# A hybrid decoder layer on one core: the DeltaNet scan without u and w formed ahead, and two groups of loads moved ahead of their splits

## The chip, the cores and the metric

The kernel runs on one core of one Trainium2 chip. The metric is the device time of one execution in microseconds (us); the time before is the median of three runs. All names of engines are those of the profile: PE is TensorE's matmul, PEld its weight load, DVE is VectorE, ACT is ScalarE, POOL is GpSimd, SP is the SyncE queue, which issues nearly all DMAs of this kernel.

## The reference

One layer over 1024 tokens of width 1024: a norm, one combined projection, two mixers side by side (gated DeltaNet with 8 heads of 128, and a sparse attention with three branches), their gated sum through an output projection, and an MLP. The part that matters is the chunked delta rule of each DeltaNet head. The reference solves for u and w ahead and then scans the chunks:

```
u = triangular_solve(t_mat, vb)                    # t_mat = 1 + strictly lower (kb k^T * decay)
w = triangular_solve(t_mat, kb * exp(gc))
qk = (q k^T) * decay ; q_dec = q * exp(gc) ; k_end = k * exp(gc_last - gc)
for each chunk:
    v_new = u_c - w_c @ state
    o     = q_dec @ state + qk @ v_new
    state = state * g_last + k_end^T @ v_new
```

Everything is float32. The merge is `sigmoid(g_dn) * (o_dn @ W_dn) + sigmoid(g_ns) * (o_ns @ W_nsa)`, which then goes through `W_out`.

## The kernel before, in words

Large products are float32 values split in two parts (hi in ACT: `act(hi, src)`; lo in DVE: `src - hi`), with three 128x512 matmuls for each 128 rows of depth. The weights of such a product come 512 columns at a time through `unit`: a DMA into `wr` (or `a22` late in the program), the two-part split into `wh` and `wl`, out of a ring of five buffers (`WB`).

The program is laid out by hand on a line of steps: `at(step, rank, fn)` collects functions, and at the end they are run in order of step and rank. A framework then keeps the program's data dependencies, and sets each engine's own order; each engine takes its instructions strictly in that order. The stages, in order of time: projection of small columns and compressed keys (to 200 us), the eight DeltaNet heads (200 to 1035 us), the sparse stage of 32 items (1035 to 1543), the merge (1543 to 1650), output projection and MLP.

A head `head(h, s0)` takes 8 steps of projection (k, q, v, gate; two halves of 512 tokens each). One half of a projection is 24 matmuls into a tile `g`: `first` does 12 of them, and `conv` (or `gate`) the other 12 and then the short convolution on DVE and ACT. Between heads stand steps of `fill` projections, which the mixers need later: `fill_nb` (sparse keys, values, queries) and `fill_rows` (merge gates, stored to `gtd`). While these matmuls run, the head's delta rule goes on in small steps in between: `k_natural`, `k_turn`, `k_k`, `k_q` prepare keys, decay and qk; `blocks` and `inv_*`, `join_*`, `last_*` invert the triangular matrices of all chunks (the inverse, transposed, is `zs`); `u_w` forms u and w for four chunks at a time; `chunk` then does one chunk of 128 tokens: two matmuls with the state (`St`) against `wq` (w and the decayed q side by side), a subtraction on DVE (`vn`), the matmul `ke` with `vn` and the state's update on DVE, the matmul `qk` with `vn`, and the output row on ACT. There are 8 chunks to a head, and chunks of one head run during the projections of the next. `out_norm` and `out_turn` norm and transpose the head's rows and store them to `odd`.

In PSUM the chunk's tiles are named `c`, in a pool of two banks (`PL.pc`), which `out_turn` takes its transposes from too. The root of a norm (`rsqrt`) is a power on POOL. The product of q and decay, half of `wq`, is on POOL as well.

In the sparse stage `dn_rows(half)` loads the DeltaNet rows (`odd`) through the two staging tiles `ra` and `rb` and splits them into `oh` and `ol`; `dn_part` multiplies them by `w_proj_dn` between the items. Its last two columns (c = 6, 7 of the second half) are done after the items, with gates `ths`. Then pools are closed and opened (`pn`, `cq` go, `pw`, `py` come), `ns_rows` loads and splits the sparse rows (`ond` into `o`), and `ns_merge` multiplies them by `w_proj_nsa` into PSUM tiles named `V`.

Of the kernel before, what the change touches and what calls it, by code (L numbers as in the profile page):

```python
# [19 lines left out]
S = 1024  # L20
# [123 lines left out]
def body(ctx: ExitStack, tc: tile.TileContext, A, out):  # L144
# [246 lines left out]
    eg = PL.cq.tile([128, 8, NT], F32, name="eg")  # L391
# [3 lines left out]
    beg = PL.cq.tile([128, 8, NT], F32, name="beg")  # L395

    def gating():
# [44 lines left out]
        act(eg, gc, AF.Exp)  # L442
        V.tensor_tensor(beg, beta, eg, OP.mult)
# [187 lines left out]
    def head(h, s0):  # L631
# [11 lines left out]
        def conv(s, half):  # L643
# [3 lines left out]
            proj(ps, H["w", s], half, (4, 8))  # L647
# [30 lines left out]
        def k_turn(half):  # L678
            sl = S4[half]
            kn = H["kn", half]  # L680
            pt = flip(kn)
            kT = t4("kT", 2)
            act(kT, pt)
            H["kT", half] = kT
            kb = t4("kbe", 2)
            rows_by(kb, kn, beg[:, h, sl])
            H["kbe", half] = kb
# [5 lines left out]
            H["qk", half] = dt = t4("qk", 3)  # L693
# [59 lines left out]
        def k_q(half):  # L753
# [3 lines left out]
            w = pd.tile([128, 4, 2, 128], F32, name="wq", bufs=2)  # L757
            GP.tensor_tensor(w[:, :, 1], ac, H["gcB"].rearrange("p (t c) -> p t c", c=128)[:, S4[half]],
                             OP.mult)
            H["wq", half] = w  # L760

        def v_natural(half):
            ps = flip(H.pop(("ac", 2, half)))
            v_ = t4("vb", 2)
# [3 lines left out]
        def first(s, half):  # L768
            H["g"] = gtile()
            proj(H["g"], H["w", s], half, (0, 4))  # L770

        def gate(half):
            ps = H.pop("g")
            proj(ps, H["w", 3], half, (4, 8))
# [62 lines left out]
        def chunk(c):  # L837
# [3 lines left out]
            o, u, St = H["o", half], H["u", half], H.get("S")  # L841
            ps = PL.pc.tile([128, 2, 128], F32, name="c")
            if St is None:
                vn = u[:, i]
            else:
                wq = H["wq", half]
                mm(ps[:, 0], wq[:, i, 0], St, True, True)
                mm(ps[:, 1], wq[:, i, 1], St, True, False)
                vn = PL.p2.tile([128, 128], F32, name="vn", bufs=2)
                V.tensor_tensor(vn, u[:, i], ps[:, 0], OP.subtract)  # L850
            if c < 7:
                p2 = PL.pc.tile([128, 128], F32, name="c")
                mm(p2, H["ke", half][:, i, :], vn, True, True)
                H["S"] = Sn = PL.p2.tile([128, 128], F32, name="St", bufs=2)
                if St is None:
                    V.tensor_copy(Sn, p2)
                else:
                    V.scalar_tensor_tensor(Sn, St, H["gl"][:, c:c + 1], p2, op0=OP.mult, op1=OP.add)
            mm(ps[:, 1], H["qk", half][:, i], vn, St is None, True)
            act(o[:, i, :], ps[:, 1], AF.Copy, scale=H["rq", half][:, i:i + 1])  # L860
# [17 lines left out]
        for i, s in enumerate((1, 0, 2, 3)):  # L878
            at(s0 + 2 * i - 2, 2, prep, s)
            for half in range(2):  # L880
                at(s0 + 2 * i + half, 1, first, s, half)
                if s < 3:
                    at(s0 + 2 * i + half + 0.5, 1, conv, s, half)
                else:
                    at(s0 + 2 * i + half + 0.5, 1, gate, half)
        for half in range(2):
# [19 lines left out]
        at(s0 + 21.2, -1, out_norm, 1)  # L906
        at(s0 + 22.2, -1, out_turn, 1)

    def fill_rows(src, dst):
# [6 lines left out]
        def begin(half):  # L916
            w[1] = gtile()
            proj(w[1], w[0], half, (0, 4))

        def go(half):  # L920
            ps = w[1]
            proj(ps, w[0], half, (4, 8))
# [5 lines left out]
        def plan(s, half):  # L928
            at(s, 1, begin, half)
            at(s + 0.5, 1, go, half)  # L930
# [3 lines left out]
    def fill_nb(u):  # L934
# [11 lines left out]

        def go(t):
            tk = slice(t * 128, (t + 1) * 128)
            ps = gtile(256)
            gemm(ps, [(hh[:, k, tk], hl[:, k, tk], w[k // 2][0][:, k % 2], w[k // 2][1][:, k % 2])  # L950
                      for k in range(8)])
# [28 lines left out]
        def plan(s, j):  # L980
            for t in (2 * j, 2 * j + 1):
                at(s + t % 2 / 2, 1, go, t)
# [8 lines left out]
    for h in range(NDN):  # L991
# [3 lines left out]
        fills = gts if h == 7 else nbs[6:] if h == 6 else [nbs[h], gts.pop(0)]  # L995
# [5 lines left out]
    END, FULL = last + 24, last + 28  # L1001
# [340 lines left out]

    def dn_rows(half):
# [28 lines left out]
    for half in range(2):  # L1372
        at3(0.2 + 16 * half, dn_rows, half)
# [16 lines left out]

    shut("pn", "cq")
# [9 lines left out]
    rows_o, mixes, ks = [], [], {}  # L1401
# [27 lines left out]
    ths = []  # L1429
    for c in (6, 7):  # L1430
        ths.append(t512(PL.pw, "a12"))
# [339 lines left out]
```

## Time and profile before

| | us |
|---|---|
| median of 3 runs (2360.64 to 2361.92) | 2360.92 |
| profiled execution: its time | 2355.1 |
| profiled execution: its span | 2353.3 |
| PE busy (98% of the span) | 2306.0 |
| DVE busy (67%) | 1567.3 |
| ACT busy (49%) | 1155.6 |
| POOL busy (8%) | 184.2 |

The profiled execution's own time is 1.8 us above its span. "Busy" counts an instruction from its start to its modelled end; matmuls overlap, so that the time one really takes of PE is the distance from its start to the next start. Idle time of PE is listed where the next matmul started after the end of the last. Engines wait on each other by semaphores; a releaser named in a row is the one whose event came last.

### The profile page before, as it was taken

To read this page: it belongs to the slowest core of one execution; us is meant where nothing else is said; L and a number is where in the kernel's file an instruction comes from. 1 tells how busy PE (TensorE), PEld (TensorE's weight loads), DVE (VectorE), ACT (ScalarE), POOL (GpSimd) and SP (SyncE) were. 2 spreads that over 40 slices of the span, in tenths; PEclk is the share of its full clock that TensorE was granted. 3 is DMA by queue.
4 is the path that set the end of the run, shared out by engine and by line. 5 is a ranking of instruction groups with operands and counts; after the bars stand their busy time and mean duration, and the time that the engine had idled before them with its cause. 6 is when DMAs were issued, how large, how long until landed. Compare 5 with 4: busy or idle time off the path is not lost.

```text
span 2353.3 us, 43197 instructions
## 1 busy us (share of the span) xinstructions
PE 2306.0 (98%) x16257; PEld 1917.6 (81%) x16257; DVE 1567.3 (67%) x3742; ACT 1155.6 (49%) x2482; POOL 184.2 (8%) x198
## 2 busy tenths in 40 slices
PE   8999999999999999999999999999999999999999
PEld 5888988888988898886777777778878888888887
DVE  7676654747574748247777777645498777787775
ACT  4335353535444454337666666532465555544443
POOL 1021210101111121000010111100000000000000
PEclk9999999999999999999999999999999999999999
DMA  6421313131213221247342422065525443595333
GB/s 196 122 62 59 81 52 96 47 89 47 84 47 84 59 74 55 82 143 184 109 128 63 122 87 66 19 220 166 174 90 179 148 148 131 189 327 185 115 114 103
DMA packets 237378, 267.28 MB, mean 114 GB/s; under 512 B 76848, under 2 KB 128496, under 8 KB 237040
## 3 DMA queue, kind: packets, MB, share of 16 engines
q1 hardware_dynamic: 237168, 264.51, 36.1%
q8 instruction: 128, 2.10, 0.4%
q14 instruction: 82, 0.67, 0.1%
HBM read 190.02 MB, written 72.38 MB: 112 GB/s over the span
## 4 chain that ended last, share of the span: by engine, by line
PE 86%; DVE 6%; DMA 2%; issue 2%; ACT 1%; POOL 1%; SPq 0%; ACTq 0%; POOLq 0%; DVEq 0%
PE g L174 31%; PE V L174 20%; PE Q L174 12%; PE T L174 5%; PE s L174 5%; PE o L174 5%; PE S L174 2%; PE c L174 2%; PE m L174 1%; POOL ss L239 1%; PE tp L606 1%; DVE wl L274 1%; PE tp L174 1%; DVE junk L1238 0%; DVE acc L659 0%
## 5 line engine op out<-in xcount | busy, mean ns | idle before, releaser
L174 PE MATMUL g<-hh,wh 128*128 128x512 f32 (+1 forms) x816 | 335.9, 412 | 6.6 <-ACT hh L171 6.5
L174 PE MATMUL g<-hl,wh 128*128 128x512 f32 (+1 forms) x816 | 322.8, 396 | 0.1
L174 PE MATMUL g<-hh,wl 128*128 128x512 f32 (+1 forms) x816 | 322.4, 395 | 0.0
L171 ACT ACTIVATE wh<-a 128x512 fp32r<-128x512 f32 x234 | 146.5, 629 | 252.9 <-PE V L174 154.4
L174 PE MATMUL V<-big,wh 128*128 128x512 f32 x768 | 236.7, 390 | 0.8 <-DVE c L1613 0.8
L1238 DVE CUSTOM_DVE_ANT_0 junk<-S,cst 128x384 f32<-128x384 f32 (+3 forms) x320 | 168.5, 533 | 57.9 <-PE S L174 53.7
L171 ACT ACTIVATE P<-T 128x512 f32<-128x512 f32 x228 | 133.8, 597 | 102.1 <-PE T L174 89.3
L174 PEld LDWEIGHTS g<-hh,wh 128*128 128x128 f32 (+1 forms) x816 | 154.1, 189 | 36.4 <-ACT hh L171 7.1
L171 ACT ACTIVATE wh<-wr 128x512 fp32r<-128x512 f32 x168 | 105.7, 629 | 158.6 <-PE g L174 126.9
L183 DVE TENSOR_TENSOR wl<-a,wh 128x512 fp32r<-128x512 f32 x192 | 132.0, 690 | 75.2 <-ACT wh L171 74.9
L174 PEld LDWEIGHTS g<-hh,wl 128*128 128x128 f32 (+1 forms) x816 | 153.8, 188 | 33.7 <-issue 0.6
L174 PEld LDWEIGHTS g<-hl,wh 128*128 128x128 f32 (+1 forms) x816 | 154.3, 189 | 28.7 <-DVE hl L327 1.5
L174 PEld LDWEIGHTS V<-big,wh 128*128 128x128 f32 x768 | 144.1, 188 | 31.4 <-DVE c L1613 1.2
L174 PE MATMUL V<-big,wl 128*128 128x512 f32 x384 | 149.5, 389 | 0.9 <-DVE wl L274 0.9
L174 PE MATMUL g<-wh,hh 128*128 128x256 f32 x512 | 148.8, 291 | 0.3 <-DVE acc L777 0.3
L174 PE MATMUL g<-wl,hh 128*128 128x256 f32 x512 | 145.4, 284 | 0.0
L174 PE MATMUL g<-wh,hl 128*128 128x256 f32 x512 | 144.7, 283 | 0.0
L174 PEld LDWEIGHTS o<-vv,P 128*64 128x64 f32 x3648 | 115.9, 138 | 27.0 <-issue 19.4
L174 PE MATMUL o<-vv,P 128*64 128x65 f32 x3648 | 129.9, 225 | 0.6 <-DVE bs L1285 0.6
L274 DVE TENSOR_TENSOR wl<-wr,wh 128x512 fp32r<-128x512 f32 x136 | 94.1, 695 | 52.5 <-ACT wh L171 46.8
L174 PE MATMUL S<-ks,qc 96*128 96x384 f32 (+3 forms) x320 | 126.4, 407 | 1.0 <-DVE mx L1238 0.4
L174 PE MATMUL Q<-big,wh 128*128 128x512 f32 x384 | 118.4, 390 | 0.7 <-ACT wh L171 0.5
(383 smaller groups left out, 5348.9 us busy)
## 6 DMA issues: line engine op xcount, KB each, us to landing
bb<-acd SPq DMA_DIRECT2D x112, 256.0 KB, 2.7
wr<-in_w_dn_dram SPq DMA_DIRECT2D x64, 256.0 KB, 3.0
a<-in_w_u_dram SPq DMA_DIRECT2D x64, 256.0 KB, 2.7
acd<-c SPq DMA_DIRECT2D x64, 256.0 KB, 2.1
a<-in_w_d_dram SPq DMA_DIRECT2D x64, 256.0 KB, 3.7
wr<-in_w_nb_dram SPq DMA_DIRECT2D x32, 256.0 KB, 2.6
wr<-in_w_gt_dram SPq DMA_DIRECT2D x32, 256.0 KB, 2.8
gtd<-fx SPq DMA_DIRECT2D x32, 256.0 KB, 2.4
```

Of the source, the lines that this page charges most:

```text
L171: return SC.activation(o, i, fn, **kw)
L174: return PE.matmul(o, l, r, start=start, stop=stop, skip_group_check=True)
L183: V.tensor_tensor(lo, src, f(hi), OP.subtract)
L239: GP.tensor_tensor(o, o, mhalf[:ss.shape[0], :n], OP.pow)
L274: V.tensor_tensor(wl, wr, f(wh), OP.subtract)
L606: PE.transpose(pt[:, i, :], src[:, i, :], ident)
L1238: V.tensor_tensor_reduce(junk[:, :w], ps[:, :w], mask[:, a:b], 1.0, 3e38, OP.add, OP.min, o)
```

## The change

In the scan, `u_w` goes, and with it the tiles `u`, `wq`, `kbe`, `beg` and `eg`. A chunk is cut in three functions. `chunk_keys` multiplies the decayed keys `kg` by the state and forms on DVE `t = beta * (kg^T S) - vb`; `chunk_values` multiplies the inverse `zs` by `t` and copies the result, negated, on ACT to `vn`; `chunk_out` does the state's matmul and update, then the two matmuls of the output. `k_q` forms `kg` and `qg` on DVE (before: the one product of q on POOL). A chunk now takes one step (before: half a step), its three functions a third of a step each, and `first` and `begin` are cut so that 9, 9 and 6 projection matmuls stand between them. `fill_nb` is cut in two in the same way. One gate projection of head 0 moves to the end of the heads. In the sparse stage the rows of half 0 are loaded whole into `ol` by `dn_load`, and split one 128-row piece at a time by `dn_split`. Before the merge, the two gates `ths` are loaded into tiles `P` of the sparse stage, and the first weights of `w_proj_nsa` into `wr`, ahead of the closing of the pools.

```
 def k_q(half):
-            w = pd.tile([128, 4, 2, 128], F32, name="wq", bufs=2)
-            GP.tensor_tensor(w[:, :, 1], ac, H["gcB"].rearrange("p (t c) -> p t c", c=128)[:, S4[half]],
-                             OP.mult)
-            H["wq", half] = w
+            for n, x in (("kg", H["kT", half]), ("qg", ac)):
+                H[n, half] = w = t4(n, 2 if n == "kg" else 3)
+                V.tensor_tensor(w, x, H["gcB"].rearrange("p (t c) -> p t c", c=128)[:, S4[half]], OP.mult)
...
-        def u_w(half):
-            u = t2("u", 2)
-            act(u, four(zs[half], H["vb", half]))
-            H["u", half] = u
-            act(H["wq", half][:, :, 0], four(H["kbe", half], zs[half]))
...
+        def chunk_keys(c):
+            half, i = c // 4, c % 4
+            H["A"] = p = PL.pc.tile([128, 2, 128], F32, name="c")
+            if c:
+                mm(p[:, 0], H["kg", half][:, i], H["S"], True, True)
+                H["t"] = t = PL.p2.tile([128, 128], F32, name="t", bufs=2)
+                V.scalar_tensor_tensor(t, p[:, 0], beta[:, h, c:c + 1], H["vb", half][:, i],
+                                       op0=OP.mult, op1=OP.subtract)
+
+        def chunk_values(c):
+            half, i = c // 4, c % 4
+            p = H["A"]
+            mm(p[:, 1], zs[half][:, i], H["t"] if c else H["vb", half][:, i], True, True)
+            H["vn"] = vn = PL.p2.tile([128, 128], F32, name="vn", bufs=2)
+            act(vn, p[:, 1], AF.Copy, scale=-1.0 if c else 1.0)
+
+        def chunk_out(c):
...
+            vn, St, k = H["vn"], H.get("S"), H["A"][:, 0]
+            p = PL.pc.tile([128, 128], F32, name="c")
             if c < 7:
+                mm(k, H["ke", half][:, i, :], vn, True, True)
                 H["S"] = Sn = PL.p2.tile([128, 128], F32, name="St", bufs=2)
+                if c:
+                    V.scalar_tensor_tensor(Sn, St, H["gl"][:, c:c + 1], k, op0=OP.mult, op1=OP.add)
                 else:
+                    V.tensor_copy(Sn, k)
+            if c:
+                mm(p, H["qg", half][:, i], St, True, False)
+            mm(p, H["qk", half][:, i], vn, c == 0, True)
+            act(H["o", half][:, i, :], p, AF.Copy, scale=H["rq", half][:, i:i + 1])
...
-            at(s0 + 15.5, 0, u_w, half)
...
         for c in range(8):
-            at(s0 + 16 + c / 2, -2, chunk, c)
-        at(s0 + 19, -1, out_norm, 0)
-        at(s0 + 20, -1, out_turn, 0)
+            for j, fn in enumerate((chunk_keys, chunk_values, chunk_out)):
+                at(s0 + 15 + (2 + j) / 3 + c + 0.001, -2, fn, c)
+        at(s0 + 20, -1, out_norm, 0)
+        at(s0 + 21, -1, out_turn, 0)
...
+    def dn_load():
+        D_["o", 0] = oh, ol = [PL.pr.tile([128, 8, 512], F32R, name=n) for n in ("oh", "ol")]
+        for k in range(0, 8, 2):
+            SY.dma_start(f(ol)[:, k:k + 2], odd[k:k + 2, :, 0:512].rearrange("a p t -> p a t"))
+
+    def dn_split(k):
+        oh, ol = D_["o", 0]
+        split(f(ol)[:, k], oh[:, k], ol[:, k])
...
+            at3(0.05, dn_load)
+            for k in range(8):
+                at3(0.7 + 0.1 * k, dn_split, k)
...
+    ths, ks = [], {}
+    for c in (6, 7):
+        ths.append(flat(PL.pr.tile([128, 4, 128], F32, name="P", bufs=6)))
+        SY.dma_start(ths[-1], gtd[c, :, 512:1024])
+    ks[0] = unit(A["w_pn"][0])
     shut("pn", "cq")
...
-        SY.dma_start(ths[-1], gtd[c, :, HALF[1]])
-    ns_rows(0, f(rows_o[1][0]), (0,))
-    ks[0] = unit(A["w_pn"][0])
-    ns_rows(0, f(rows_o[1][0]), (1, 2, 3))
+    ns_rows(0, f(rows_o[1][0]), range(4))
```

Over the whole program the change takes 64 matmuls of 128x128x128 out of PE's list (16 in `u_w` of each head go, 8 net come back in its chunks), 16 products off POOL and 32 onto DVE, and 64 row products (`kbe`) and 32 copies off ACT with 64 copies (`vn`) onto it.

Where the instructions now stand is seen at three places. First PE in the scan, in the second head. Before, one chunk's rows (`c` are the chunk's PSUM tiles, `g` the projection's):

```order
L174 MATMUL c<-St,wq 128x128 [waits DVE_49,Activation_49]
L174 MATMUL c<-St,wq 128x128 [waits Pool_49]
L174 MATMUL g<-hh,wh 128x512
L174 MATMUL g<-hl,wh 128x512
L174 MATMUL g<-hh,wl 128x512
L174 MATMUL g<-hh,wh 128x512
L174 MATMUL g<-hl,wh 128x512
L174 MATMUL g<-hh,wl 128x512
L174 MATMUL c<-vn,ke 128x128 [waits DVE_49]
L174 MATMUL c<-vn,qk 128x128
```

In the change, the end of chunk 5 in the same head; nine rows of `g` stand between its `kg` row and its `zs` row, and nine between `zs` and `ke`. In `out_turn`, four transposes `c<-cst,o` of half 0 stand behind chunk 5's `kg` row and take the second bank of the pool.

```order
L174 MATMUL g<-hh,wl 128x512
L174 MATMUL c<-vn,ke 128x128 [waits Activation_49]
L174 MATMUL c<-St,qg 128x128 [waits DVE_49]
L174 MATMUL c<-vn,qk 128x128
L174 MATMUL g<-hh,wh 128x512
L174 MATMUL g<-hl,wh 128x512
L174 MATMUL g<-hh,wl 128x512
L174 MATMUL g<-hh,wh 128x512
L174 MATMUL g<-hl,wh 128x512
L174 MATMUL g<-hh,wl 128x512
L174 MATMUL c<-St,kg 128x128 [waits DVE_49]
```

The wait for DVE has moved: from `ke`, with six `g` ahead of it, to `qg`, with one matmul ahead of it, and to `kg`, with six. In the other chunks the `qg` row waits for nothing. Second ACT, in the same head, where `out_norm` of half 0 falls between the chunks (`oss` is the root from POOL). Before:

```order
L171 ACTIVATE o<-c,rq 128x128 [waits DVE_49,PE_49]
L171 ACTIVATE o<-o,oss 128x128 [waits Activation_49,Pool_49]
L171 ACTIVATE o<-o,oss 128x128 x3
L171 ACTIVATE acc<-xp,cols 128x512 [waits DVE_49]
L171 ACTIVATE o<-c,rq 128x128 [waits DVE_49,PE_49]
```

In the change, ahead of chunk 4's `ke`:

```order
L171 ACTIVATE of<-o 128x512 [waits DMAHW7_49,Activation_49]
L171 ACTIVATE wh<-wr 128x512 [waits DMAHW7_49,PE_49]
L171 ACTIVATE acc<-xp,cols 128x512 [waits DVE_49]
L171 ACTIVATE o<-o,oss 128x128 [waits Activation_49,Pool_49]
L171 ACTIVATE o<-o,oss 128x128 x3
L171 ACTIVATE vn<-c 128x128 [waits PE_49]
```

What moved there is `vn`: it was made on DVE, and now stands on ACT behind four rows that wait for POOL; before, an output row stood behind them, for which no matmul of the chunk waits. Third SP's queue ahead of the merge. Before:

```order
L1432 DMA a_18588<-gtd 128x512 [waits DVE_49,PE_49,Pool_49]
L1297 DMA ond<-ot 128x2x128 [waits DMAHW5_49,Activation_49]
L1432 DMA a_18590<-gtd 128x512 [waits DMAHW6_49]
L1409 DMA o<-ond 128x2x512 [waits DMAHW7_49]
L284 DMA a_18597<-in_w_pn_dram 128x512 [waits DMAHW0_49]
L284 DMA a_18603<-in_w_pn_dram 128x512 [waits DMAHW1_49]
L1409 DMA o<-ond 128x2x512 [waits DMAHW2_49]
```

In the change (the two loads of `w_pn` stand eight rows and more ahead of this):

```order
L1420 DMA P<-gtd 128x512 [waits DMAHW6_49,PE_49,Activation_49]
L1420 DMA P<-gtd 128x512 [waits DMAHW7_49,PE_49,Activation_49]
L1440 DMA o<-ond 128x2x512 [waits DVE_49,DMAHW0_49,PE_49,Pool_49]
L1309 DMA ond<-ot 128x2x128 [waits DMAHW1_49,Activation_49]
L1440 DMA o<-ond 128x2x512 [waits DMAHW2_49]
```

The wait for the closed pools (DVE, PE and POOL together) was at the first gate's load and is now at the first load of sparse rows; two gates and two weights of 256 KB each no longer stand in its way.

## Rows read from the trace of the kernel before

**Rows 1.** The page: the span, and the busy time of PE, DVE and POOL.

```profile
span 2353.3 us, 43197 instructions
PE 2306.0 (98%) x16257; PEld 1917.6 (81%) x16257; DVE 1567.3 (67%) x3742; ACT 1155.6 (49%) x2482; POOL 184.2 (8%) x198
```

**Rows 2.** Who PE waited for, over the whole span: us in total, times, longest.

```profile
PE c L174 <- DVE vn L850: 9.2, 13, 0.8
...
PE c L174 <- DVE xp L652: 4.4, 6, 0.8
PE V L174 <- ACT o L171: 2.9, 1, 2.9
PE V L174 <- DVE wl L274: 2.6, 2, 1.7
```

**Rows 3.** PE in order of time, `u_w` of the second head: start, us, instruction, count. One 128x128x128 float32 product is two instructions.

```profile
314.60 1.05 PE L174 MATMUL s<-vb,zs 128*128 128x128 f32 x8
315.48 1.06 PE L174 MATMUL s<-zs,kbe 128*128 128x128 f32 x8
316.38 1.11 PE L174 MATMUL s<-vb,zs 128*128 128x128 f32 x8
317.33 1.06 PE L174 MATMUL s<-zs,kbe 128*128 128x128 f32 x8
318.14 0.48 PE L174 MATMUL g<-hh,wh 128*128 128x512 f32 x1
```

**Rows 4.** PE in order of time, one chunk of the same head. In square brackets: idle before, and its releaser.

```profile
324.62 0.61 PE L174 MATMUL c<-St,wq 128*128 128x128 f32 x4
324.98 0.48 PE L174 MATMUL g<-hh,wh 128*128 128x512 f32 x1
325.30 0.39 PE L174 MATMUL g<-hl,wh 128*128 128x512 f32 x1
...
326.23 0.40 PE L174 MATMUL g<-hh,wl 128*128 128x512 f32 x1
327.29 0.49 PE L174 MATMUL c<-vn,ke 128*128 128x128 f32 x2 [0.67 <-DVE vn L850]
```

**Rows 5.** DVE in order of time, the same chunk and the next ones.

```profile
324.58 0.17 DVE L238 TENSOR_SCALAR ss<-ss 128x4 f32<-128x4 f32 x1
...
326.35 0.69 DVE L675 TENSOR_TENSOR nat<-tp,ss 128x512 f32<-128x512 f32 x1 [0.90 <-POOL ss L239]
326.96 0.28 DVE L850 TENSOR_TENSOR vn<-u,c 128x128 f32<-128x128 f32 x1
...
327.82 0.35 DVE L858 SCALAR_TENSOR_TENSOR St<-St,gl,c 128x128 f32<-128x128 f32 x1
...
337.00 1.69 DVE L694 TENSOR_TENSOR qk<-dm,cst 128x512 f32<-128x512 f32 x1
...
347.93 0.17 DVE L238 TENSOR_SCALAR oss<-oss 128x4 f32<-128x4 f32 x1
```

**Rows 6.** POOL in order of time: the product that makes half of `wq`.

```profile
336.83 1.30 POOL L758 TENSOR_TENSOR wq<-acc,gcB 128x512 f32<-128x512 f32 x1 [1.67 <-PE c L174]
```

**Rows 7.** ACT in order of time: the output row of a chunk, and `out_norm`'s four products.

```profile
347.89 0.37 ACT L171 ACTIVATE o<-c,rq 128x128 f32<-128x128 f32 x1 [1.89 <-PE c L174]
349.59 1.28 ACT L171 ACTIVATE o<-o,oss 128x128 f32<-128x128 f32 x4 [1.33 <-POOL oss L239]
```

**Rows 8.** Busy time by stretch in the scan of that head: stretch, its us, then PE, PEld, DVE, ACT, POOL (instructions), granted clock, DMA share, GB/s.

```profile
336.00:342.00 6.00, 5.01 (x35) 4.56 (x35) 5.63 (x12) 5.14 (x15) 1.30 (x1) 1.00 0.12 44
...
324.00:366.00 42.00, 39.84 (x232) 33.91 (x230) 33.31 (x78) 21.44 (x50) 8.61 (x7) 1.00 0.20 58
```

**Rows 9.** PE in order of time at the merge. `T` is the last column of `w_proj_dn`, `V` the merge's products.

```profile
1551.15 0.39 PE L174 MATMUL T<-oh,wl 128*128 128x512 f32 x1
1554.39 0.76 PE L174 MATMUL V<-o,wh 128*128 128x512 f32 x2 [2.86 <-ACT o L171]
...
1557.93 0.81 PE L174 MATMUL V<-o,wh 128*128 128x512 f32 x2
...
1563.83 0.50 PE L174 MATMUL V<-o,wl 128*128 128x512 f32 x1 [1.66 <-DVE wl L274]
```

**Rows 10.** The merge's loads on SP (start and length of the issue), and the first of ACT and DVE that they and the gates feed.

```profile
1543.17 0.33 SPq L1432 DMA_DIRECT2D a<-gtd  x1
...
1545.33 0.43 SPq L1409 DMA_DIRECT2D o<-ond  x1
1550.53 1.15 ACT L171 ACTIVATE o<-o 128x512 fp32r<-128x512 f32 x2 [7.01 <-DMA o<-ond]
...
1553.61 0.68 DVE L1368 SCALAR_TENSOR_TENSOR a<-a,T 128x512 f32<-128x512 f32 x1
```

**Rows 11.** Busy time by stretch at the merge (columns as in rows 8).

```profile
1546.00:1550.00 4.00, 4.00 (x19) 3.31 (x18) 0.69 (x1) 0.00 (x0) 0.00 (x0) 1.00 0.96 236
1550.00:1554.00 4.00, 1.53 (x7) 0.94 (x5) 2.81 (x5) 3.04 (x6) 0.00 (x0) 1.00 1.05 401
1554.00:1558.00 4.00, 3.61 (x10) 2.87 (x11) 3.90 (x7) 2.61 (x5) 0.00 (x0) 0.61 0.95 323
...
1562.00:1566.00 4.00, 2.34 (x10) 1.80 (x10) 3.73 (x7) 2.38 (x5) 0.00 (x0) 1.00 1.05 401
```

**Rows 12.** The sparse stage where `dn_rows` loads half 0: ACT at a split, and the matmul behind it on PE.

```profile
1085.14 1.06 ACT L171 ACTIVATE oh<-ra 128x1024 fp32r<-128x1024 f32 x1 [1.19 <-DMA ra<-odd]
...
1086.73 0.50 PE L174 MATMUL T<-qd,kd 128*128 128x512 f32 x1 [1.01 <-ACT P L171]
```

More of the change, by code (lines that the diff above doesn't have):

```diff
@@ L646, in conv @@
             ps = H.pop("g")
-            proj(ps, H["w", s], half, (4, 8))
+            proj(ps, H["w", s], half, (6, 8))
             xp = pd.tile([128, 515], F32, name="xp", bufs=2)
@@ L692, in k_turn @@
             V.tensor_tensor(ut, H["gcB"].rearrange("p (t c) -> p t c", c=128)[:, sl], b3(gc[:, h, sl]), OP.subtract)
-            H["qk", half] = dt = t4("qk", 3)
+            H["qk", half] = dt = t4("qk", 4)
             V.tensor_tensor(dt, ut, bm("m2"), OP.add)
@@ L880, in head @@
             for half in range(2):
-                at(s0 + 2 * i + half, 1, first, s, half)
+                for k in (0, 3):
+                    at(s0 + 2 * i + half + k / 9, 1, first, s, half, k)
                 if s < 3:
-                    at(s0 + 2 * i + half + 0.5, 1, conv, s, half)
+                    at(s0 + 2 * i + half + 2 / 3, 1, conv, s, half)
                 else:
-                    at(s0 + 2 * i + half + 0.5, 1, gate, half)
+                    at(s0 + 2 * i + half + 2 / 3, 1, gate, half)
         for half in range(2):
@@ L914, in prep, with begin @@
             w[0] = unit(src)
-        def begin(half):
-            w[1] = gtile()
-            proj(w[1], w[0], half, (0, 4))
+        def begin(half, k):
+            if k == 0:
+                w[1] = gtile()
+            proj(w[1], w[0], half, (k, k + 3))
         def go(half):
             ps = w[1]
-            proj(ps, w[0], half, (4, 8))
+            proj(ps, w[0], half, (6, 8))
             x = PL.pf.tile([128, 512], F32, name="fx", bufs=2)
@@ L928, in plan @@
         def plan(s, half):
-            at(s, 1, begin, half)
-            at(s + 0.5, 1, go, half)
+            at(s, 1, begin, half, 0)
+            at(s + 1 / 3, 1, begin, half, 3)
+            at(s + 2 / 3, 1, go, half)
         return prep, [lambda s, i=i: plan(s, i) for i in range(2)]
@@ L945, in prep, with part, begin @@
                 w.append((wh, wl))
+        def part(ps, t, ks):
+            tk = slice(t * 128, (t + 1) * 128)
+            for k in ks:
+                wh, wl = [a[:, k % 2] for a in w[k // 2]]
+                mm(ps, hh[:, k, tk], wh, k == 0, False)
+                mm(ps, hh[:, k, tk], wl, False, False)
+                mm(ps, hl[:, k, tk], wh, False, k == 7)
+        def begin(t):
+            X["g"] = gtile(256)
+            part(X["g"], t, range(4))
         def go(t):
             tk = slice(t * 128, (t + 1) * 128)
-            ps = gtile(256)
-            gemm(ps, [(hh[:, k, tk], hl[:, k, tk], w[k // 2][0][:, k % 2], w[k // 2][1][:, k % 2])
-                      for k in range(8)])
+            ps = X.pop("g")
+            part(ps, t, range(4, 8))
             x = PL.p2.tile([128, 256], F32, name="nx", bufs=4)
@@ L981, in plan @@
             for t in (2 * j, 2 * j + 1):
-                at(s + t % 2 / 2, 1, go, t)
+                at(s + t % 2 / 2, 1, begin, t)
+                at(s + t % 2 / 2 + 0.25, 1, go, t)
                 if u not in (2, 3):
@@ L994, in body @@
         s += 8
-        fills = gts if h == 7 else nbs[6:] if h == 6 else [nbs[h], gts.pop(0)]
+        fills = gts if h == 7 else nbs[6:] if h == 6 else nbs[:1] if h == 0 else [nbs[h], gts.pop(0)]
         for prep_, go_ in fills:
@@ L1000, in body @@
                 s += 1
-    END, FULL = last + 24, last + 28
+    END, FULL = last + 26, last + 30
     def tail_b():
@@ L1372, in body @@
     for half in range(2):
-        at3(0.2 + 16 * half, dn_rows, half)
+        if half:
+            at3(16.2, dn_rows, 1)
+        else:
+            at3(0.05, dn_load)
+            for k in range(8):
+                at3(0.7 + 0.1 * k, dn_split, k)
         for c in range(8):
@@ L1399, in t512 @@
         return p.tile([128, 512], F32, name=name, **({} if bufs is None else dict(bufs=bufs)))
-    rows_o, mixes, ks = [], [], {}
+    rows_o, mixes = [], []
     for half in range(2):
```

43 lines of the change are left out of this document (8 added, 35 removed).

## The prediction

> **What bounds the kernel now.** I read the page first: PE is busy 2306.0 of a span of 2353.3 us [rows 1], so an instruction taken out of PE's list shortens the kernel by about the time it takes there, if PE then doesn't wait in its place. What remains is PE's idle time, 47 us. The list of whom PE waited for gives its causes [rows 2]: 13.6 us in 19 waits of the scan's matmuls for DVE (9.2 + 4.4; the row that names `xp` is a tiny fill beside the same `vn`), and two waits at the merge, 2.9 and 1.7. Then PE in order of time at the places that the change touches. Two products in a row of the scan cost PE 324.98 - 324.62 = 0.36, and the first projection matmul behind them 0.32 where it takes 0.23 in a row (four distances from 325.30 to 326.23), together 0.45, 0.22 for each float32 product [rows 4]; the 16 products of `u_w` give the same, (318.14 - 314.60) / 16 = 0.22 [rows 3]. There is no fixed price for going to and fro between the two kinds, so that it costs nothing in itself that the change cuts a chunk in three groups. A stall of the scan costs more than its listed idle: from 326.23 the next matmul was due at 326.46 and started at 327.29, 0.83 for an idle of 0.67 [rows 4]. So the 19 waits cost 13.6 + 19 x 0.16 = 16.6 us.
>
> Why these stalls are there is read from DVE: it stood 0.90 us idle for a root from POOL, then did `nat` (0.69), then `vn` [rows 5], and PE had only six projection matmuls (1.4 us) to cover it. DVE is the engine to watch, since in the scan's stretch it is busy 33.3 of 42 us, in one stretch 5.63 of 6 [rows 8].
>
> **The change, part by part.** *Matmuls.* 128 products of `u_w` go and 64 net come back in the chunks (a head has 5 in a chunk, but 3 in the first and 4 in the last, 37; before 16 + 29 = 45). 64 x 0.22 = **-14.2 us**, on PE and so on the path.
>
> *Waits of the scan.* The chain from state to state gets longer: `kg` product, DVE, `zs` product, ACT, `ke` product, DVE, three handoffs where there were two. But `kg` to `zs` and `zs` to `ke` now have nine matmuls of cover, 2.1 us, and `ke` to the next `kg` two products and six, 1.8 us. A handoff over DVE needs about 0.9: from the start of `ke` at 327.29 [rows 4] to the end of the state's update at 327.82 + 0.35 [rows 5] is 0.88. So an undisturbed chunk doesn't wait. Three places aren't undisturbed, by the change's order:
>
> First, in chunk 5 of every head `qg` waits for DVE with only `ke` ahead of it. The transposes of `out_turn` have taken the second of two banks, so the output's tile is in the bank that the state's update has yet to read. `qg` can start 0.88 after `ke` instead of 0.22: 0.66 at least, and up to 0.69 more when DVE is in a row of 128x512 (`nat`'s size [rows 5]). I take 0.7 x 8 heads = 5.6.
>
> Second, in chunk 4 `vn` stands on ACT behind the four products of `out_norm`, which wait for POOL. From the end of the scaled sum on DVE (347.93 + 0.17 [rows 5]) to these products are 1.49 us, they take 1.28, and a row like `vn` 0.37 [rows 7]: 3.1 us, against a cover of 2.1 from `zs` on. The sum is formed a little earlier than `zs`. Between 0 (formed early) and 1.5 (the whole root in the way), I take 0.8, the middle, in the seven heads whose scan runs beside a next head: 5.6.
>
> Third, the state's update of chunk 1 stands on DVE behind `nat` and its root, as `vn` did: between 0 and the 0.83 that this cost before [rows 4], I take 0.5 x 7 = 3.5.
>
> Together 14.7 in place of 16.6: **-1.9 us**. Elsewhere the cover hides the handoffs; without it each would cost 0.7 (0.88 less a product).
>
> *DVE's new rows.* `kg` and `qg` are four rows of 0.69 to a head, 2.8 us; `t` has the form of the state's update, 0.35 for `vn`'s 0.28, 0.5 more. They lie beside the projections: 33.3 + 3.3 of 42 less the 2 that PE saves. POOL's product goes: at 336.83 it took 1.30 [rows 6], and a DVE product of two SBUF tiles that began at 337.00 took 1.69, 1.0 more than its kind [rows 5], so it gives DVE back between 0 and 2 us a head. I charge DVE's new rows at nothing beyond the three places; the rival below has the price if that cover is gone.
>
> The Trainium skill says the same of those rows ("SBUF — State Buffer", section "Who interferes with whom"): a DVE instruction with two SBUF inputs and a GpSimd instruction that reads SBUF take one shared port in turn, whoever starts first keeping it for the whole instruction. It speaks against the change too: `kg` and `qg` have two SBUF inputs and can now be held up by each of POOL's roots. By that rule DVE is held up about as often as before, with the sum unchanged; the rows above agree with the lock, and none of them shows what a root of POOL does to a DVE row.
>
> *ACT* loses 8 rows of `kbe` and four copies of four chunks a head and gets eight `vn`: less work, nothing on the path but `vn` itself.
>
> *The merge.* After the last `T` (1551.15, next due at 1551.38) PE waited until 1554.39, 3.0 us [rows 9]. Then it ran slow: nine matmuls took 1557.93 - 1554.39 = 3.5 us where 2.1 is due [rows 9], with a granted clock of 0.61 [rows 11], which mixes the lower level of 1.2 GHz with the full 2.4; 1.5 lost. Then a stall of 1.66, or 1.8 with its margin. Sum 6.3. The wait came from the sparse rows: their load was issued at 1545.33, 2.2 us after the queue could go on at 1543.17, and landed for ACT at 1550.53 [rows 10]. Now it is issued first, with 1 MB of gates and weights no longer around it. But the first `V` waits for one more thing, as the order of the change shows: behind it the lo parts of six pieces are used without a wait, so its own wait on DVE is for the row after these, the gate's product on the last `T`, which held 0.68 at 1553.61 [rows 10]. That can't start before `T` ends at 1551.54. So `V` starts at 1552.3 at best, and at 1554.39 - 2.2 = 1552.2 if only the load counts; with some lateness of the third load I take 1552.6, 1.2 us lost. After 1.66 idle the stretch still shows a clock of 1.00, after 2.86 it shows 0.61 [rows 11], so I expect no slow stretch: 3.0 + 1.5 - 1.2 = 3.3 gained (between 4.0 and, with a slow stretch and the third load late, 0.7). What is late next: the second half's sparse rows now stand behind weights whose buffers wait for DVE, and eight lo rows of DVE must keep pace with PE. I put the later stall at 1.5 for the 1.8 before (0 to 3.5). Merge **-3.6 us**.
>
> *Sparse stage.* ACT stood 1.19 us idle for a load of DeltaNet rows, and PE 1.01 for the exponentials queued behind it [rows 12]. Now four loads go out together, earlier, and the splits stand behind four exponentials. The same 2 MB moves, and later loads of queries stand behind it. Between -1.9 and +1, I take **-1.0 us**. Second half, fills and `gating` (two small rows fewer): nothing.
>
> **Sum.** -14.2 - 1.9 - 3.6 - 1.0 = -20.7 us. The profiled execution took 2355.1 (its span 2353.3 and 1.8 around it), 5.8 under the median of the runs; I expect 2334.4 of its like, and against the median 2360.92 - 20.7 = **2340 us**.
>
> **Rivals.** *Everything covered.* Only chunk 5's wait stays (0.66 x 8 = 5.3), and merge and sparse stage give their best (4.0 and 1.3 of the later stall's 1.8, and 1.9): -14.2 - 11.3 - 5.3 - 1.9 = -32.7, 2328 us. For it: nine matmuls of cover are 1.2 more than a handoff needs. Against: the three places above are in the order.
>
> *Only the matmuls count.* The three places cost their upper bounds in most heads (1.35 x 8 + 1.5 x 7 + 0.8 x 7 = 27), and the merge stalls again: -14.2 + 10 - 3 or so, 2350 to 2356. For it: DVE's waits for POOL are still in its order. A milder form, stalls as before and half of the merge, gives 2346.
>
> *DVE becomes the bound (slower).* Place: the chunks beside k's and q's convolutions, where DVE was busy 5.63 of 6 us [rows 8] and now gets `kg` and `qg`, 1.4 us more, in the same stretch. Then `t` is late in chunk after chunk, and DVE doesn't catch up. It decides from stalls of 16.6 + 14.2 + 4.6 = 35.4 us, 5 in each of seven heads, 0.63 a chunk; at 0.75 more a chunk than I have (7 x 8 x 0.75 = 42) the time is 2382. Against: over the stretch of 42 us DVE has some 9 us left, and PE's own waits shrink with it. The port rule of the skill named above would feed this one.
>
> **How the numbers follow.** My sum with errors of some 5 us (2335 to 2346) 45%; all covered, 2326 to 2335, 20%; only the matmuls, 2346 to 2356, 24%; no change within 0.2% 5%; DVE the bound, slower, 6%. About 0.2% (4.7 us) is what a measurement of this kernel can tell from no change. Range for 8 in 10: 2328 to 2354, which leaves out 2% below the best case and the slower ones above. Faster 0.88, same 0.05, slower 0.07.
>
> **What would show it.** PE's matmul count less by 128 instructions, and no `s<-vb,zs`. In the list of PE's waits: a wait of `c` for DVE `St` of 0.4 to 0.6, eight times (chunk 5); one for ACT `vn` up to 1.3 in up to seven heads; none for `t`. Waits for `t` in many chunks would show DVE as the bound. At the merge: one idle of about 1 us ahead of the first `V`, released by DVE, and a granted clock of 1.00 behind it; a second one of 1 to 2 us when the second half's rows begin. ACT not idle for `odd` loads of half 0. The prediction is wrong if the sum of PE's idle in the scan is over 20 us, or if merge's first `V` still comes 3 us behind `T`.

## The result, and the profile after

The change took the median from 2361.28 us (four runs, 2360.64 to 2361.92) to 2327.41 (four runs, 2323.56 to 2337.11): a ratio of 0.9863, 95% interval 0.9833 to 0.9893. A second series of four gave 2329.19 and 0.9879 (0.9857 to 0.9901). So 30 to 34 us are gained where 21 were forecast; the time is just below the range's low end of 2328, and in the second series just above it. Medians and ratios here and below leave out one slow run, of the kernel with other banks (5269.98 us). The profiled execution took 2327.88 us, 27.2 less than that of before. From here on sums are made between the profiled executions.

The page after, its span and busy times, beside [rows 1]:

```profile
span 2326.0 us, 42906 instructions
PE 2288.1 (98%) x16129; PEld 1904.3 (82%) x16129; DVE 1580.3 (68%) x3777; ACT 1138.2 (49%) x2453; POOL 165.6 (7%) x182
```

PE has the 128 instructions less. Whom it waited for, beside [rows 2] (us in total, times, longest):

```profile
PE V L174 <- ACT o L171: 3.3, 2, 3.1
PE c L174 <- ACT vn L171: 3.1, 6, 1.3
...
PE c L174 <- DVE St L851: 1.2, 6, 0.3
PE V L174 <- DVE wl L274: 0.9, 1, 0.9
...
PE V L174 <- DVE o L183: 0.7, 1, 0.7
```

The scan's waits fell from 13.6 us to 4.3, and none is for `t`. The merge's long wait is still there. Three marks on PE tell where the time went: the first `T` (a projection behind the heads, shortly ahead of the sparse items), the last `T`, and the first `V`. The first `T`, before and then after:

```profile
1043.02 0.39 PE L174 MATMUL T<-hh,wh 128*128 128x512 f32 x1
```

```profile
1012.38 0.39 PE L174 MATMUL T<-hh,wh 128*128 128x512 f32 x1
```

| start on PE, us | before | after | difference | the part gained |
|---|---|---|---|---|
| first `T` (end of the heads) | 1043.02 | 1012.38 | -30.6 | heads -30.6 (forecast -16.1) |
| last `T` [rows 9] | 1551.15 | 1524.24 | -26.9 | sparse stage +3.7 (forecast -1.0) |
| first `V` [rows 9] | 1554.39 | 1527.76 | -26.6 | |
| end of the span | 2353.3 | 2326.0 | -27.3 | merge and all behind it -0.4 (forecast -3.6) |

The heads gave nearly twice the forecast, and the moved loads nothing. The heads again, as the sum of PE's distances from start to start between 195 us and the first `T`, with the part of a distance that a listed wait makes (over the usual distance) taken out:

| us | before | after | difference |
|---|---|---|---|
| products of the scan (360 before, 296 after) | 77.5 | 55.4 | -22.1 |
| projection matmuls, the same number | 634.3 | 638.9 | +4.6 |
| all other matmuls | 118.3 | 115.6 | -2.7 |
| waits (those of the scan: 16.9 and 6.4) | 17.8 | 7.4 | -10.4 |

**The three places of the scan.** Chunk 5 of the second head, PE and then DVE in order of time:

```profile
350.10 0.38 PE L174 MATMUL c<-vn,ke 128*128 128x128 f32 x2
350.32 0.39 PE L174 MATMUL c<-St,qg 128*128 128x128 f32 x2
...
350.58 0.33 DVE L851 SCALAR_TENSOR_TENSOR St<-St,gl,c 128x128 f32<-128x128 f32 x1
```

`qg` started 0.22 behind `ke`, ahead of the state's update. So its wait for DVE in the order was not for that update; it had been met before. Chunk 4 (POOL, ACT, PE) and chunk 1 (DVE, PE) of the same head:

```profile
339.93 1.01 POOL L239 TENSOR_TENSOR oss<-oss,mhalf 128x4 f32<-128x4 f32 x1 [3.77 <-DVE oss L238]
340.97 1.28 ACT L171 ACTIVATE o<-o,oss 128x128 f32<-128x128 f32 x4 [1.99 <-POOL oss L239]
342.16 0.25 ACT L171 ACTIVATE vn<-c 128x128 f32<-128x128 f32 x1
342.46 0.49 PE L174 MATMUL c<-vn,ke 128*128 128x128 f32 x2 [0.35 <-ACT vn L171]
...
315.92 0.69 DVE L671 TENSOR_TENSOR nat<-tp,ss 128x512 f32<-128x512 f32 x1 [0.90 <-POOL ss L239]
317.72 0.34 DVE L851 SCALAR_TENSOR_TENSOR St<-St,gl,c 128x128 f32<-128x128 f32 x1
318.21 0.46 PE L174 MATMUL c<-St,kg 128*128 128x128 f32 x2 [0.18 <-DVE St L851]
```

Here both mechanisms are as forecast: `vn` behind four rows that waited for POOL's root, the update behind `nat` and its root, which PE meets at the next `kg`. Each is small: 0.35 and 0.18 listed.

**The start of the sparse stage.** PE's first mask product of the items; one load of the stage's set-up on SP, before; the same load after, with SP's rows ahead of it; and, after, the busy time by stretch (columns as in [rows 8]):

```profile
1021.15 0.35 PE L174 MATMUL m<-far,gsel 128*128 128x256 f32 x1 [1.35 <-issue]
```

```profile
1040.05 0.60 SPq L1050 DMA_DIRECT2D junk<-in_kcc_dram  x1
```

```profile
1008.42 0.42 SPq L872 DMA_DIRECT2D odd<-of  x1
1011.02 0.33 SPq L284 DMA_DIRECT2D wr<-in_w_pd_dram  x1
...
1014.01 0.33 SPq L925 DMA_DIRECT2D gtd<-fx  x1
...
1014.87 0.47 SPq L1062 DMA_DIRECT2D junk<-in_kcc_dram  x1
```

```profile
1044.00:1048.00 4.00, 3.51 (x13) 2.11 (x13) 3.61 (x21) 3.94 (x11) 0.12 (x1) 0.84 0.45 130
1048.00:1052.00 4.00, 3.24 (x16) 2.66 (x14) 2.23 (x5) 1.27 (x9) 0.00 (x0) 0.73 0.09 25
1052.00:1056.00 4.00, 3.09 (x22) 2.08 (x23) 2.88 (x13) 3.92 (x12) 0.00 (x0) 0.70 0.93 304
1056.00:1060.00 4.00, 4.00 (x12) 2.78 (x12) 2.04 (x9) 1.99 (x5) 0.73 (x1) 0.50 1.05 320
```

That load was issued 3.0 us ahead of the first `T` before (1043.02 - 1040.05), and 2.5 behind it after. PE then waited six more times for 0.2 us or more in the next 35 us, and its mean granted clock was between 0.84 and 0.50 (0.50 is the 1.2 GHz level) in four stretches.

**The merge.** PE at the last `T` and the first `V`; ACT's splits of the sparse rows; DVE:

```profile
1524.24 0.39 PE L174 MATMUL T<-oh,wl 128*128 128x512 f32 x1
1527.76 0.96 PE L174 MATMUL V<-o,wh 128*128 128x512 f32 x2 [3.13 <-ACT o L171]
...
1520.61 1.16 ACT L171 ACTIVATE o<-o 128x512 fp32r<-128x512 f32 x2 [3.69 <-DMA o<-ond]
...
1525.11 1.15 ACT L171 ACTIVATE o<-o 128x512 fp32r<-128x512 f32 x2 [1.85 <-DMA o<-ond]
...
1525.77 1.29 DVE L183 TENSOR_TENSOR o<-o 128x512 fp32r<-128x512 f32 x2 [1.70 <-ACT o L171]
1526.98 0.68 DVE L1389 SCALAR_TENSOR_TENSOR P<-P,T 128x512 f32<-128x512 f32 x1
```

The first load did come earlier: its split began 3.6 us ahead of the last `T`, before 0.6 ahead [rows 9, 10]. But the gate's product on `T` stands on DVE behind the lo rows of the third load, and that landed only at 1525.11. `V` started 0.10 behind the end of this product (1526.98 + 0.68), as it did before (1553.61 + 0.68 = 1554.29, and 1554.39 [rows 9, 10]). PE had been idle for 3.13, and a stretch at the lower clock followed, as before (0.61 [rows 11]):

```profile
1528.00:1532.00 4.00, 4.00 (x12) 3.09 (x12) 1.55 (x3) 0.99 (x2) 0.00 (x0) 0.57 0.74 232
```

### The profile page after: what moved, and what is told of

It is laid out like the page before. It is cut to its first block, busy times and chain, and to the rows that moved or that the text cites. A ratio compares the mean times of both kernels' runs of the same rounds, so it can differ in the third digit from the quotient of the medians.

```text
span 2326.0 us, 42906 instructions
## 1 busy us (share of the span) xinstructions
PE 2288.1 (98%) x16129; PEld 1904.3 (82%) x16129; DVE 1580.3 (68%) x3777; ACT 1138.2 (49%) x2453; POOL 165.6 (7%) x182
## 4 chain that ended last, share of the span: by engine, by line
PE 85%; DVE 7%; DMA 3%; ACT 2%; issue 2%; POOL 1%; SPq 0%; ACTq 0%; POOLq 0%; DVEq 0%
PE g L174 30%; PE V L174 20%; PE Q L174 12%; PE T L174 5%; PE o L174 5%; PE s L174 4%; PE c L174 2%; PE S L174 2%; PE m L174 1%; DVE acc L655 1%; PE tp L602 1%; POOL ss L239 1%; PE tp L174 1%; DVE wl L274 0%; PE tp L982 0%
## 5 line engine op out<-in xcount | busy, mean ns | idle before, releaser
L174 PEld LDWEIGHTS g<-hl,wh 128*128 128x128 f32 (+1 forms) x816 | 154.6, 189 | 27.3 <-DVE hl L327 0.8
L174 PEld LDWEIGHTS o<-vv,P 128*64 128x64 f32 x3648 | 116.3, 138 | 26.6 <-issue 19.8
```

The source lines that it names most:

```text
L174: return PE.matmul(o, l, r, start=start, stop=stop, skip_group_check=True)
```

## The experiments

Unless told otherwise a kernel has the change's scan and projection cut, with sparse stage and merge as before ("the scan alone"). Where an edit only reverses part of the change, it is told in words.

**The scan alone** (the diff without `dn_load`, `dn_split` and the early `ths` and `ks[0]`).

> The change's scan and projection cut alone; sparse stage and merge load as before. Theory A (the gain is all in the heads, the moved loads cost): in the profile the first product of the sparse stage's first projection comes 30 to 31 us earlier than before, the last T of the merge too, and the end 30 to 31 earlier, some 3 us better than the whole change in its profile. Theory B (the recorded reasons: the moved loads gain 4.6, the heads give 16 to 25): the end comes 16 to 25 earlier, and this kernel is some 4 us slower than the whole change.

2328.76 us, ratio 0.9863 (0.9851 to 0.9876); span 2325.1. Heads -30.8, the sparse stage 1.6 longer than before, the merge and all behind it 1.0, so that the end came 28.2 earlier. Theory A holds for where the gain is: all of it is the heads'. Its sizes don't: the end was to come 30 to 31 earlier and the kernel to be some 3 better than the whole change, from which its median can't be told (2327.41 and 2329.19). The moved loads are worth nothing in sum. The sparse stage lost without them too, though ACT no longer stood idle for the DeltaNet rows of half 0 in either kernel ([rows 12]: 1.19 before).

**The whole change without its merge loads.**

> The whole change but for the merge, whose gates and first weights are loaded as before. Theory A (the early load of DeltaNet rows costs 3 to 4 us in the sparse stage, and the moved merge loads give nothing): from the first product of the sparse stage's projection to the last T of the merge 3 to 4 us more than before, the merge as before within 0.5, the end 26 to 28 us earlier than before. Theory B (the early load gains 1, the merge's loads 3.6): the sparse stage 1 us shorter, and this kernel 3.6 us slower than the whole change.

2330.97, 0.9874 (0.9861 to 0.9887). Heads -29.4, sparse stage +6.1, last `T` to first `V` +0.4. As theory A has it in direction; in size the sparse stage lost more than its 3 to 4, and the end came 22.5 earlier, not 26 to 28.

**The old scan at the new pace** (before, with):

```
-            at(s0 + 16 + c / 2, -2, chunk, c)
+            at(s0 + 16 + c + 0.001, -2, chunk_in, c)
+            at(s0 + 16 + c + 1 / 3 + 0.001, -2, chunk_out, c)
```

where `chunk_in` has the two products with `wq` and `vn`, and `chunk_out` the rest; the projection cut of the change, `wq` three and `qk` four deep, and `kbe` written over `nat` to make room.

> The scan of before (u and w formed ahead, 64 more products), but with a chunk to a whole step and 9 to 12 projection matmuls between the subtraction's product and ke, where before had 6; sparse stage and merge as before. Theory A (the cover alone takes the scan's waits away): PE's listed waits for vn fall from 13.6 us to under 2, the heads get shorter by 13 to 17 us. Theory C (a wait for DVE's root and row is not a matter of cover, it moves to the next product): waits stay over 8 us, the heads get shorter by under 5.

2364.31, 1.0014 (1.0004 to 1.0024); the heads got 5.2 us longer, where theory C had them up to 5 shorter. Its reason holds: PE still waited for `vn`, and now for two more.

```profile
PE c L174 <- DVE vn L849: 10.1, 15, 1.9
...
PE c L605 <- ACT o L171: 3.5, 6, 0.6
PE tp L605 <- DVE acc L662: 2.8, 5, 0.6
```

One wait for `vn`, in order of time (POOL, DVE, PE):

```profile
341.67 1.47 POOL L756 TENSOR_TENSOR wq<-acc,gcB 128x512 f32<-128x512 f32 x1 [7.43 <-PE c L174]
341.90 1.95 DVE L708 TENSOR_TENSOR n<-dm,cst 64x256 f32<-64x256 f32 x2
343.10 1.19 POOL L239 TENSOR_TENSOR rq<-rq,mhalf 128x4 f32<-128x4 f32 x1
344.32 0.17 DVE L748 TENSOR_SCALAR rq<-rq 128x4 f32<-128x4 f32 x1 [0.47 <-POOL rq L239]
344.40 0.28 DVE L849 TENSOR_TENSOR vn<-u,c 128x128 f32<-128x128 f32 x1
344.83 0.46 PE L174 MATMUL c<-vn,ke 128*128 128x128 f32 x2 [0.71 <-DVE vn L849]
```

`vn` stood on DVE behind a row that waits for POOL's root, and the root stood on POOL behind the product. Eleven projection matmuls between `wq` and `ke` were no cover for that.

**The new scan at the old pace** (`16 + c / 2 + (0, 1, 3)[j] / 8`, the projection cut by single rows of depth).

> The scan of the change at the old pace: a chunk in half a step, so that only 3 projection matmuls (0.68 us) stand between kg's product and zs, and 6 between zs and ke; sparse stage and merge as before. Theory A (64 products fewer give about 14 to 17 us, and the new chain needs its cover of nine): the products' gain stays, but waits for t of 0.2 to 0.4 in most chunks and some longer ones, 20 to 35 us in all, so the heads are between 8 us shorter and 12 us longer than before. Theory C (the shorter list of products is all that matters): heads 14 to 17 us shorter, waits as in the change.

2341.14, 0.9919 (0.9906 to 0.9932); heads -16.7. The products' gain stays in the main, and the waits are 14.4 us of the heads (17.8 before). Theory C has the size, but not the waits; theory A's waits for `t` were 1.5 us in two places, not 20 to 35. So products and pace each give about half, and the pace only together with the new chain. Of the 14 us between this kernel and the scan alone some 7 are waits (14.4, and 7.4 in the change); the projection is also cut finer here.

**`vn` on DVE.**

```
-            act(vn, p[:, 1], AF.Copy, scale=-1.0 if c else 1.0)
+            V.tensor_scalar(vn, p[:, 1], -1.0 if c else 1.0, None, op0=OP.mult)
```

> The change's scan (sparse stage and merge loads as before), with one row moved: vn is copied out of PSUM by DVE, where the change has ACT. Cover and products stay. Theory A (nine projection matmuls of cover hide any handoff): PE's waits for vn in the heads stay at 3 to 4.5 us, the heads within 2 us of the same kernel with vn on ACT. Theory D (what counts is that vn stands on an engine whose order has no rows that wait for POOL's roots): waits for vn of 0.4 to 0.8 come back in two or three chunks of each head that runs beside the next one's projections, 7 to 15 us in all, and the heads get longer by as much; the waits of 0.3 to 1.6 behind out_norm's rows on ACT go.

2341.06, 0.9914 (0.9895 to 0.9932). The first `T` comes 13.6 us later than with `vn` on ACT, at the same products and the same cover; 2.5 of this are there at the first `s<-kT` product (124.22 for 121.70), before any chunk has run, so that some 11 are the scan's. Theory D:

```profile
PE c L174 <- DVE vn L839: 6.9, 12, 2.1
PE c L174 <- DVE xi L719: 4.5, 5, 0.9
```

All twelve waits for `vn` have the same cause: a row on DVE that waited 0.9 to 1.2 us for a root of POOL stood ahead of `vn`. In the second head:

```profile
313.59 0.69 DVE L671 TENSOR_TENSOR nat<-tp,ss 128x512 f32<-128x512 f32 x1 [0.90 <-POOL ss L239]
...
314.86 0.28 DVE L839 TENSOR_SCALAR vn<-c 128x128 f32<-128x128 f32 x1
```

The five waits listed under `xi` are for the state: its update stood on DVE behind a row that waited for ACT, and ACT had stood in `out_norm`'s rows, behind their root.

**`qg` back on POOL** (`kg` on DVE).

> The change's scan (sparse stage and merge loads as before), with qg's product back on POOL, kg's stays on DVE. Theory E (POOL's product takes a DVE row's port time and stands ahead of a root that DVE waits for): beside the product one DVE row with two SBUF inputs a head takes 0.7 to 1.4 more than its kind, roots behind it come 1.2 to 1.5 later, and new PE waits of 3 to 10 us in the heads make it slower by as much. Theory A (DVE has the room): DVE busy 10 us less, PE's waits as with qg on DVE within 1.5 us, no change in time.

2333.70, 0.9886 (0.9869 to 0.9904). The heads are 1.7 longer than in the scan alone, with 5.6 us of idle in the scan's waits for 4.6. The rest of the difference lies in the sparse stage, which the edit doesn't touch. Of theory E the delay is seen, and its price is small: 1 us of waits for its 3 to 10. DVE's busy time did not fall, as theory A had it.

**Other PSUM banks for `V`** (the scan alone, the change's merge loads, the pools closed in the order that this needs, and):

```
-        for n, b in (("S", 2), ("T", 2), ("m", 2), ("o", 1)):
+        for n, b in (("m", 2), ("o", 1), ("S", 2), ("T", 2)):
```

> The change's scan and its early gates and weights at the merge (sparse rows of DeltaNet as before), and PSUM's pools of the sparse stage opened in another order, so that the four banks of V are not those of T. Theory F (the first V waits for the gate's product on the last T, because V's bank lies over T's): the first V comes within 0.6 us of the last T's end, no stretch at the lower clock follows, the merge is 4 to 5 us shorter than in the whole change. Theory G (opening V's pool waits for every reader of the closed pools): the first V still starts 0.1 us behind the gate's product on T, 2 to 3.5 us behind T.

2326.87 (three runs), 0.9858 (0.9837 to 0.9878). Theory G: the gate's product ended at 1524.94 + 0.68, and `V` started 0.10 later. And a later wait took what the first gave:

```profile
1524.94 0.68 DVE L1380 SCALAR_TENSOR_TENSOR P<-P,T 128x512 f32<-128x512 f32 x1
...
1525.72 0.70 PE L174 MATMUL V<-o,wh 128*128 128x512 f32 x2 [2.78 <-ACT o L171]
1540.65 1.90 PE L174 MATMUL V<-o,wh 128*128 128x512 f32 x5 [3.77 <-ACT o L171]
```

**`out_norm` later** (`s0 + 20` to `s0 + 20.1`), and then **its transposes later too** (`s0 + 21` to `s0 + 21.4`).

> The change's scan (sparse stage and merge loads as before), with out_norm of half 0 a tenth of a step later, so that chunk 4's vn stands ahead of its four rows on ACT. Theory (the vn waits are those rows waiting for POOL's root): PE's six waits for vn, 3.4 us listed, are gone or under 0.5, the heads 3.5 to 4.5 us shorter. Rival (the root's delay moves on to the next vn or to the transposes): other waits of the same sum appear, no change.

> The change's scan (sparse stage and merge loads as before), with out_norm of half 0 a tenth of a step later and its transposes 0.4 of a step later. Theory (the root's delay can be hidden wholly, it only needs both places): neither waits for vn nor waits of the transposes for o, PE's listed waits in the heads under 2 us, 3 to 4.5 us less than the change's scan. Rival (it moves on to the next product again): waits of about 3.5 us elsewhere, no change.

2329.19 (0.9867) and 2328.21 (0.9868), both as the scan alone. The waits for `vn` are gone in both; in the first the transposes wait instead, in the second for the state, 2.1 us:

```profile
PE c L602 <- ACT o L171: 3.7, 6, 0.9
```

```profile
PE c L602 <- DVE St L851: 2.1, 6, 0.4
```

So the rival holds: the root's delay moves on, and shrinks by 1.3 us at most (3.4 in the scan alone, 2.1 here).

**The sparse stage one step later** (the whole change, `FULL = last + 31`), beside **the whole change once more**.

> The whole change, with all of the sparse stage behind its set-up one step of projection later against the heads (one number, FULL; the fills that follow cover it). Theory H (the stretched scan of the last head closes its pools one step before the set-up's loads, where before it had nearly two, so the stage's first mask product waits, and PE then runs at its lower clock for a stretch): the wait of 1.2 to 4.3 us ahead of the first product of far and gsel goes, and from the first T to the tenth item the stage takes 122 to 124 us in place of 126, the time falls by 2 to 4 us. Rival (the waits of the first items are the loads of DeltaNet rows that compete for the DMA engines): that stretch stays at 126, no change.

> The whole change once more, beside the three others of this batch. Expected: 2324 to 2331, as the change's scan alone (2328.8 beside 2360.3 before), since the moved loads were worth nothing in sum.

2327.80 (0.9867) and 2329.19 (0.9879): no difference. From the first `T` to the tenth item it is 126.0 us with the edit, 126.2 and 127.0 without. The wait ahead of the mask product fell to 0.86, and one for the next load came up:

```profile
1032.52 0.71 PE L174 MATMUL m<-kcb,qn 128*128 128x128 f32 x4 [2.49 <-DMA qn<-nsd]
```

The remedy of theory H fails. Its observation stands in the issue times: in the new scan at the old pace, whose last head is done earlier, the same load was issued 13.8 us ahead of the first `T`, no wait stood ahead of the mask product, and the stretch took 121.6 us (before 122.2). Of the kernels at the new pace none is under 123.1. So an early set-up goes with a short stretch; that the late one is the cause is not shown.

**All that seemed to help** (scan alone, both rows of half 0 later, the merge loads, `FULL + 1`).

> All that helped, together: the change's scan with out_norm and transposes of half 0 later, the merge's gates and weights loaded ahead as in the change, DeltaNet rows as before, the sparse stage one step later. If the parts add: 4 from the heads, 2 to 4 from the sparse stage, 0.5 from the merge: 2319 to 2323, better than the whole change by 5 to 9. If the waits only move: as the whole change within 2.

2325.35 (2324.91 to 2326.81), 0.9859 (0.9837 to 0.9882). Its four runs all lie below the four of the whole change beside it (2328.28 to 2334.91), 3.8 us between the medians; less than the parts' sum had it. Against the whole change's first series (2323.56 to 2337.11) no gain is clear.

## Why the prediction was right and wrong

**Direction and main term: right.** 64 products fewer: -22.1 of the products and +4.6 of the projections' matmuls, cut more often, make -17.5 where 14.2 was forecast: 0.27 for each product less, not 0.22. "Costs nothing in itself" held, and more: the 128 products of `u_w` took 28.4 at 0.22 each, so that the 64 that came back cost some 11, 0.17 each, with all that the finer cut costs.

**Waits of the scan: the term that was mis-sized.** 14.7 was charged, 6.4 measured. Chunk 5's wait of `qg`, 5.6 of it, did not exist: the step that failed took a wait mark in the order for the state's update, though the order doesn't tell for which DVE instruction a wait is. Chunk 4's `vn`: 4.1 us (five times 0.5, once 1.5) where 5.6 stood, in six heads, not seven; chunk 1's update: 2.2 where 3.5 stood, in five heads, with one wait in chunk 3 of a sixth. What was argued, nine matmuls of cover, is only half of the reason for the gain: with `vn` on DVE the cover was the same, and PE's listed waits in the scan were 12.2 us for 4.6. The other half, that `vn` left the engine whose order holds the rows that wait for POOL, the prediction mentioned only as a danger on ACT. Neither half does it alone: the heads gained 30.8 with both, 16.7 with `vn` on ACT at the old pace, and 17.3 with `vn` on DVE at the new one (19.4 counted from the first `s<-kT` product).

**DVE's new rows at nothing: right.** DVE is busy 13 us more, and PE never waited for `t`. That rival (slower) is out. `kg` and `qg` took 0.67 to 0.70 in every head: no root of POOL held them up.

**The inverse: not foreseen.** 2.7 us of the heads went from matmuls outside the scan; waits for `za`'s loads in two heads (four, 1.5 us listed) that are gone are a part of it.

**Sparse stage: wrong sign.** -1.0 was forecast from the DeltaNet rows' load, and "second half, fills and `gating`: nothing". What was left out is the end of the last scan. One fill moved behind the heads, so that the last head begins two steps earlier, but its last transposes come at its step 25 and no longer at 22.2: 0.8 of a step nearer to the stage's set-up, whose pools they hold. Its load was issued 5.5 us later against PE's work. The transposes make up 2.7 of this (8.6 us ahead of the first `T` before, 5.9 after). The rest came in SP's own order: behind the store of the transposed rows (1008.42) stood a load of weights that waited for DVE until 1011.02 and a gate's store that waited for ACT until 1014.01, and the set-up's load only then. The new scan at the old pace, transposes at 22.2, two steps earlier than before, had the load early and no wait; since an edit that moved the items a step later gave nothing, the cause of the loss is argued, not shown. Its size fits the slower clock in the stretches behind the waits: 4 x (0.16 + 0.27 + 0.30 + 0.50) = 4.9 us as an estimate, if PE had work all along, against 1.7 before (0.70 and 0.87 in two stretches of 4). What the early load of DeltaNet rows itself does stays open: 126.0 to 127.0 in four profiles with it, 123.1 to 127.7 in five without.

**Merge: wrong.** The first `V` was to start 1.2 us behind `T`; it started 3.3 behind where it was due. The dependence was named rightly (the gate's product on `T`), and "some lateness of the third load" was taken as 0.3: it was 2.4. So the 1.5 for the stretch at the lower clock, which the sum took as gained, was not: it stayed (0.57). In the profiles of all these kernels `V` starts 0.10 to 0.11 behind this product, and what is gained there can go again at the second half's rows (3.77 us in the kernel with other banks). The condition "wrong if the first `V` still comes 3 us behind `T`" was met; the one on the scan's idle (over 20 us) was not.

So the total of *everything covered* (2328) came out by other terms than its own: the heads gave 30.6 where its sum has 25.5 (14.2 + 11.3), merge and sparse stage lost 3.3 where it has a gain of 7.2.

## What to carry to other kernels

When a chain runs from engine to engine beside other work, ask on which engine's in-order list each link stands and what that list waits for, before counting its cover: here eleven matmuls did not cover a link that stood behind POOL's root. The right engine alone didn't do it either; it took both. A wait mark in an order is not yet a wait: look for what it waits on and when that was done. And when work is stretched over more steps to hide it, its end moves too: price what starts behind the last round, and what stands ahead of it in the queue.

## What the runs showed of the hardware

A DVE copy of three elements to a partition took 1.12 us beside POOL's product (POOL from 334.26 for 1.30 us, `qg` on POOL), 0.16 in the change; in five heads it took 1.11 to 1.17, each time until the product's end:

```profile
334.47 1.12 DVE L646 COPY xp<-xp 128x3 f32<-128x3 f32 x1
```

The prediction had expected that only of rows with two SBUF inputs. The Trainium skill ("SBUF — State Buffer", section "Who interferes with whom") says that a copy too can take the port pair that DVE shares with GpSimd, and is then blocked for the whole of the other's instruction; the row agrees. With POOL's roots no such block is seen: 30 DVE rows of two SBUF inputs, in the kernel before and in the change, began while the record has a root running, and all took their usual time. One case of the kernel before, the first of two rows of a kind that takes 0.41 to 0.42:

```profile
344.55 1.01 POOL L239 TENSOR_TENSOR rq<-rq,mhalf 128x4 f32<-128x4 f32 x1 [6.41 <-DVE rq L238]
345.25 0.85 DVE L710 TENSOR_TENSOR n<-dm,cst 64x256 f32<-64x256 f32 x2
```

The same code of the sparse stage's start took 123.1 to 127.7 us in five kernels that differ only in the heads, depending on when its waits fell and how long PE's clock stayed low behind them (the granted clock over the stretch was 0.99 in the shortest and 0.95 in the longest). A single profile can't price an edit of 2 us there.
